# SWA bias table in 128 partitions instead of 16, and its 1 MB store from there

## The chip, the cores and the metric

The kernel runs on one core of a Trainium2 chip. The metric is the device time of one execution in microseconds. Before the change it is 2172.07 us, the median of three runs (2171.89 to 2172.37).

## The reference

One layer of a streaming encoder in float32: 1024 prompt tokens and 64 sample tokens, width 1024. A projection gives the inputs of two branches, retention (4 heads) and sliding-window attention (SWA, 16 heads, each chunk of 64 queries against 192 keys). Their gated sum is followed by cross-attention and a SwiGLU. The change is in the SWA branch's relative-position bias, which is the same for every chunk:

```python
bucket = jnp.where(rel > 0, half, 0) + jnp.where(n < max_exact, n, large)
b = table[bucket]                       # table: 32 buckets x 16 heads
s = s + bias.astype(jnp.float32)        # 16 heads x 64 queries x 192 keys
```

The bias depends only on key position minus query position, which takes 255 values. So one row of 255 numbers for each head holds all of it.

## The kernel before, in words

All large matmuls are made from a high and a low part of each operand, three products each. The projections of the first stage go through a seven-product scheme (`strassen`, with the matmuls on lines 223, 224 and 226, the DVE sums on lines 274 and 613, and the splits into parts on lines 124 and 125). Head by head, `project_phase` projects keys, queries, values and, from head 1 on, one pair of SWA query tiles (`w_sq`). It stores them in DRAM and runs `retention(h)`. This takes four blocks of 256 tokens and the 64 sample tokens. Each block loads ks, vf and qs from `d_qkv`, turns ks and vf on TensorE (line 768), makes scores `pss` (lines 157 to 159), the state's update `pkv` and the output `po`. A scheduler mixes these with the projections of the next matrix, in an order fixed when the program is built.

`bias_table` is put on the list `self.later` behind `retention(1)`, and is emitted by the next matmul group that empties this list. It does the following.

- Line 570 and 571 load the table (32 buckets by 16 heads) and a 32x256 matrix with a one in the bucket of each distance.
- Line 573 multiplies them: row h of `pb` is the bias of head h at the 255 distances.
- Line 574 scales by 8 and writes it twice in a row, into `rb`, 512 columns in 16 partitions.
- Line 575 stores it to `d_rb` in DRAM, 64 copies of the row of 256 for each head. The source is the 16 partitions, each read 32 times by a stride of zero: 512 pieces of 2 KB, 1 MB in all.
- Lines 579 to 585 spread the sinks with a further matmul.

Much later `begin_swa` (line 1116) reads `d_rb` back with a row stride of 255 instead of 256, by which each query's row is shifted by one.

Loads and stores of this stage are all issued by SP (`load`, line 118, `store`, line 121), one behind another in a fixed order. Each also waits for the DMA issued some eight before it that has the same semaphore (DMAHW0 to DMAHW7). POOL multiplies the SWA query tiles by the norm (line 619) ahead of their stores to `d_sq`, two stores for each tile: one of 128x8x64 and one of 128x32.

These are SP's rows from the bias store on, in the program before. Behind each stands what the instruction waits for; the names are the tiles of this section, and stage holds the SWA query tiles.

```order
153 L121 DMA d_rb<-rb 512x1x512 [waits DMAHW6_49,DVE_49]
154 L121 DMA d_sq<-stage_640 128x32 [waits DMAHW7_49,Pool_49]
155 L121 DMA d_sq<-stage_640 128x8x64 [waits DMAHW0_49]
156 L121 DMA d_sq<-stage_640 128x32 [waits DMAHW1_49,Pool_49]
157 L121 DMA d_sq<-stage_640 128x8x64 [waits DMAHW2_49]
158 L118 DMA vf<-d_qkv 128x2x256 [waits DMAHW3_49,PE_49]
159 L121 DMA d_sq<-stage_640 128x8x64 [waits DMAHW4_49,Pool_49]
160 L121 DMA d_sq<-stage_640 128x32 [waits DMAHW5_49]
161 L118 DMA raw<-w_q 128x1024 [waits DMAHW6_49,DVE_49]
162 L118 DMA ks<-d_qkv 128x2x256 [waits DMAHW7_49,PE_49]
163 L118 DMA qs<-d_qkv 128x2x256 [waits DMAHW0_49]
```

The load of w_q in row 161 has the semaphore of the bias store in row 153. With the change these rows read the same, each at its place.

Of the kernel before, what the change touches and what calls it, by code (L numbers as in the profile page):

```python
# [11 lines left out]
F32 = mybir.dt.float32  # L12
F32R = mybir.dt.float32r
AF = mybir.ActivationFunctionType
ALU = mybir.AluOpType
# [4 lines left out]
P = 128  # L20
# [7 lines left out]
BLK = 256  # L28
# [81 lines left out]
class Kernel:  # L110
# [453 lines left out]
    def bias_table(self):  # L564

        nc, io = self.nc, self.io
        t = self.ra.tile([P, BLK + 16], F32, tag="sf", bufs=1, name="table")
        rb = self.ra.tile([P, 2, BLK], F32, tag="o", bufs=1, name="rb")[:16]
        table, onehot = t[:32, BLK:], t[:32, :BLK]
        self.load(table, io["rel_bias"])  # L570
        self.load(onehot, io["c_onehot"])
        pb = self.norm_psum("pb")
        nc.tensor.matmul(pb[:16, :256], table, onehot, start=True, stop=True)
        nc.vector.tensor_scalar(rb, pb[:16, :256].unsqueeze(1).broadcast_to([16, 2, 256]), 8.0, None, ALU.mult)
        self.store(self.d_rb.rearrange("h (i c) -> h i c", c=512),
                   rb.rearrange("p a b -> p (a b)").unsqueeze(1).broadcast_to([16, 32, 512]))
        row = self.np.tile([P, 16], F32, tag="row", bufs=1, name="row")[:1]
        self.load(row, io["sinks"])
        ps = self.norm_psum("ps")
        nc.tensor.matmul(ps[:, :16], self.ones[:1, :], row, start=True, stop=True)  # L580
        for e in range(2):
            rows = slice(e * 64, (e + 1) * 64)
            nc.vector.tensor_copy(self.sinks[rows, :], ps[rows, :16].rearrange("p (a b) -> p a b", b=2)[:, :, e])
        self.minus = self.np.tile([P, 16], F32, tag="row", bufs=1, name="minus")[:, :NPAIR]
        nc.vector.tensor_scalar(self.minus, self.sinks, -1.0, None, ALU.mult)
# [1307 lines left out]
```

## Time and profile before

| | |
|---|---|
| median of the runs | 2172.07 us |
| profiled execution | 2170.14 us |
| its span, first to last instruction | 2168.3 us |
| mean granted clock of TensorE | 0.996 |
| PE, DVE, ACT, POOL busy | 98%, 71%, 40%, 27% |
| DMA: moved, mean rate | 290.84 MB, 134 GB/s |
| bias store issued, landed after | 306.5 us, 12.7 us |

Times in the profile are microseconds from the start of the span. PE is TensorE's matmul, PEld its loading of the stationary operand, DVE VectorE, ACT ScalarE, POOL GpSimd, and SPq the DMA issues on SP's queue. A row of the timeline has start, duration, engine, line, operation, output and inputs, and in brackets how long the engine had been idle and what released it. A row of a table of stretches has the stretch, its length, busy time of PE, PEld, DVE, ACT and POOL with the number of instructions, the granted clock, the busy share of the 16 DMA engines, and GB/s.

### The profile page before, as it was taken

The page shows a single profiled execution, that of the slowest core. Times are in us where ns is not written, and L with a number is a line of the kernel's source. Part 1 is how long each engine was busy: PE and PEld are TensorE (multiplying, and loading weights), DVE is VectorE, ACT ScalarE, POOL GpSimd, SP SyncE. Part 2 cuts the span into 40 slices and gives each one's busy share as a digit, 9 for nine tenths or more (in the row PEclk, how much of TensorE's full clock was granted, in tenths as well). Part 3 has the DMA queues.
Part 4 walks back from the last instruction along what each step waited for, and adds up shares of the span by engine and source line. Part 5 has one row for each costly group of instructions (what it writes and reads, how often), then busy time and mean ns, then how long its engine had stood idle before and what let it go on. Part 6 is the DMA issues. An engine that isn't in the chain of part 4 may idle for free. (4 is left out here: it accounts for less than half of the span.)

```text
span 2168.3 us, 41740 instructions
## 1 busy us (share of the span) xinstructions
PE 2134.6 (98%) x16371; PEld 2082.8 (96%) x16371; DVE 1547.7 (71%) x2874; ACT 875.0 (40%) x1896; POOL 588.8 (27%) x484
## 2 busy tenths in 40 slices
PE   9999999999999999999999999999999999999997
PEld 9999999999999997889999999999999999999997
DVE  8986978776677558656545565778777777877597
ACT  8333434353434357543233333333322222344243
POOL 0001211233253124540000000015556555523531
PEclk9999999999999999999999999999999999999998
DMA  7334453444345476336442121522342333384333
GB/s 268 118 128 120 135 140 104 138 126 154 120 142 178 154 228 218 119 108 209 133 147 96 40 69 46 161 67 91 126 149 89 105 117 100 117 311 151 112 116 112
DMA packets 169894, 290.84 MB, mean 134 GB/s; under 512 B 39298, under 2 KB 96546, under 8 KB 169698
## 3 DMA queue, kind: packets, MB, share of 16 engines
q1 hardware_dynamic: 161666, 269.00, 38.8%
q0 software_dynamic: 3424, 10.82, 1.4%
q10 hardware_dynamic: 4608, 8.36, 1.0%
q8 instruction: 129, 2.11, 0.4%
q14 instruction: 67, 0.55, 0.1%
HBM read 196.95 MB, written 91.16 MB: 133 GB/s over the span
## 5 line engine op out<-in xcount | busy, mean ns | idle before, releaser
L125 DVE TENSOR_TENSOR wq<-raw,wq 128x512 fp32r<-128x512 f32 (+1 forms) x499 | 435.4, 877 | 131.8 <-ACT wq L124 128.2
L124 ACT CAST wq<-raw 128x512 fp32r<-128x512 f32 (+1 forms) x499 | 301.8, 614 | 539.8 <-PE pq L226 210.5
L224 PE MATMUL pq<-T,wq 128*128 128x272 f32 x1832 | 492.2, 289 | 0.1
L223 PE MATMUL pq<-T,wq 128*128 128x272 f32 x1832 | 490.7, 288 | 1.3 <-DVE stage L613 0.6
L224 PE MATMUL pq<-B,wq 128*128 128x272 f32 x1592 | 427.0, 288 | 0.1
L223 PE MATMUL pq<-B,wq 128*128 128x272 f32 x1592 | 425.7, 288 | 0.0
L226 PE MATMUL pq<-T,wq 128*128 128x272 f32 x1832 | 382.9, 289 | 1.9 <-DVE wq L125 1.9
L223 PEld LDWEIGHTS pq<-T,wq 128*128 128x128 f32 x1832 | 344.4, 188 | 2.1 <-ACT xsq L499 0.8
L224 PEld LDWEIGHTS pq<-T,wq 128*128 128x128 f32 x1832 | 344.2, 188 | 1.2 <-issue 0.8
L226 PE MATMUL pq<-B,wq 128*128 128x272 f32 x1592 | 331.7, 289 | 0.0
L224 PEld LDWEIGHTS pq<-B,wq 128*128 128x128 f32 x1592 | 299.1, 188 | 0.8 <-issue 0.4
L223 PEld LDWEIGHTS pq<-B,wq 128*128 128x128 f32 x1592 | 299.0, 188 | 0.1
L226 PEld LDWEIGHTS pq<-T,wq 128*128 128x128 f32 x1832 | 289.8, 189 | 3.9 <-DVE wq L125 2.4
L201 POOL TENSOR_TENSOR raw<-raw 128x512 f32<-128x512 f32 (+1 forms) x44 | 62.2, 1413 | 802.4 <-DVE rs_r L322 455.6
L226 PEld LDWEIGHTS pq<-B,wq 128*128 128x128 f32 x1592 | 251.7, 189 | 0.9 <-issue 0.7
L274 DVE TENSOR_TENSOR u<-pq,u 128x544 f32<-128x544 f32 x177 | 127.2, 719 | 84.8 <-PE pq L226 84.6
L619 POOL TENSOR_TENSOR stage<-stage,rstd 128x544 f32<-128x544 f32 x20 | 31.6, 1584 | 323.0 <-ACT rstd L514 203.7
L613 DVE TENSOR_TENSOR stage<-pq,u 128x544 f32<-128x544 f32 x112 | 80.3, 718 | 31.6 <-PE pq L226 27.8
L157 PE MATMUL pd<-xc,wq 128*128 128x256 f32 (+1 forms) x256 | 74.5, 291 | 0.0
L1541 POOL TENSOR_TENSOR stage<-stage,rstd_f 128x544 f32<-128x544 f32 x40 | 63.9, 1607 | 39.1 <-ACT stage L1540 39.1
L159 PE MATMUL pd<-xc,wq 128*128 128x256 f32 (+1 forms) x256 | 74.1, 290 | 0.0
L158 PE MATMUL pd<-xc,wq 128*128 128x256 f32 (+1 forms) x256 | 73.7, 288 | 0.0
(391 smaller groups left out, 4587.2 us busy)
## 6 DMA issues: line engine op xcount, KB each, us to landing
hl<-d_op SPq DMA_DIRECT2D x85, 272.0 KB, 5.1
d_qkv<-stage SPq DMA_DIRECT2D x44, 272.0 KB, 2.2
d_op<-stage SPq DMA_DIRECT2D x44, 272.0 KB, 2.5
d_op<-ht SPq DMA_DIRECT2D x44, 272.0 KB, 3.6
raw<-w_gate SPq DMA_DIRECT2D x22, 512.0 KB, 3.5
raw<-w_up SPq DMA_DIRECT2D x22, 512.0 KB, 5.1
raw<-w_down SPq DMA_DIRECT2D x16, 512.0 KB, 4.9
d_gate<-stage ACTq DMA_DIRECT2D x28, 272.0 KB, 2.8
```

The source lines that it names most:

```text
L124: self.last_cast = self.nc.scalar.copy(hi, src).ins
L125: return self.nc.vector.tensor_tensor(out=lo, in0=src, in1=hi.bitcast(F32), op=ALU.subtract).ins
L157: mm(ps, wh, xh, start=start, stop=False)
L158: mm(ps, wh, xl, start=False, stop=False)
L159: self.last_mm = mm(ps, wl, xh, start=False, stop=stop).ins
L201: tt(out=a11, in0=a11, in1=a21, op=sub)
L223: mm(ps[:, c, :HC], w[:, 0, ks], x[:, 0, cs], start=start, stop=False)
L224: mm(ps[:, c, :HC], w[:, 0, ks], x[:, 1, cs], start=False, stop=False)
L226: self.last_mm = mm(ps[:, c, :HC], w[:, 1, ks], x[:, 0, c * HC:(c + 1) * HC], start=False, stop=stop).ins
L274: add = lambda out, a, b: nc.vector.tensor_tensor(out=out, in0=a, in1=b, op=ALU.add)
L613: nc.vector.tensor_tensor(out=o, in0=ps, in1=sb, op=ALU.add)
L1541: nc.gpsimd.tensor_tensor(out=g, in0=g, in1=r[t], op=ALU.mult)
```

## The change

The host repeats each of the 16 columns of the table eight times, so the table is 32x128. The matmul then gives 128 rows, eight alike for each head, and DVE scales them all. In the store partition 8h + r supplies four of the 32 pieces of head h. The same bytes go to the same places of `d_rb`, in the same 512 pieces of 2 KB.

```diff
-        t = self.ra.tile([P, BLK + 16], F32, tag="sf", bufs=1, name="table")
-        rb = self.ra.tile([P, 2, BLK], F32, tag="o", bufs=1, name="rb")[:16]
+        t = self.ra.tile([P, BLK + P], F32, tag="sf", bufs=1, name="table")
+        rb = self.ra.tile([P, 2, BLK], F32, tag="o", bufs=1, name="rb")
...
-        nc.tensor.matmul(pb[:16, :256], table, onehot, start=True, stop=True)
-        nc.vector.tensor_scalar(rb, pb[:16, :256].unsqueeze(1).broadcast_to([16, 2, 256]), 8.0, None, ALU.mult)
-        self.store(self.d_rb.rearrange("h (i c) -> h i c", c=512),
-                   rb.rearrange("p a b -> p (a b)").unsqueeze(1).broadcast_to([16, 32, 512]))
+        nc.tensor.matmul(pb[:, :256], table, onehot, start=True, stop=True)
+        nc.vector.tensor_scalar(rb, pb[:, :256].unsqueeze(1).broadcast_to([P, 2, 256]), 8.0, None, ALU.mult)
+        self.store(self.d_rb.rearrange("h (r i c) -> (h r) i c", r=8, i=4),
+                   rb.rearrange("p a b -> p (a b)").unsqueeze(1).broadcast_to([P, 4, 512]))
...
-    arr["rel_bias"] = a["rel_bias"]
+    arr["rel_bias"] = np.repeat(a["rel_bias"], 8, axis=1)
```

On the engines the instructions keep their number and their order. Three differ in shape. On PE, in the place shown here, the matmul of line 573 has 128 rows:

```order
 L223 MATMUL pq<-T_250,wq 128x272
 L902 MATMUL pb<-ident,ret_o 128x64 x2
-L573 MATMUL pb<-table 16x256
+L573 MATMUL pb<-table 128x256
 L224 MATMUL pq<-T_250,wq 128x272
 L226 MATMUL pq<-T_250,wq 128x272 x2
```

The neighbours are the same matmuls as before. The scaling of line 574 on DVE writes 128x512 instead of 16x512, and the load of line 570 brings 32x128 instead of 32x16.

## Prediction

> **What bounds the kernel now.** I read the page's first part, then the waits of TensorE, then the stretch around the bias table in order of time.
>
> ```profile
> PE 2134.6 (98%) x16371; PEld 2082.8 (96%) x16371; DVE 1547.7 (71%) x2874; ACT 875.0 (40%) x1896; POOL 588.8 (27%) x484
> ```
>
> TensorE is busy for 2134.6 of 2168.3 us. Only 34 us are idle, so the change can matter only where it makes or removes idle time of PE. The waits of PE, longest in total first:
>
> ```profile
> engine line waited for: us in total, times, longest us
> PE pss L1006 <- DVE nm L1016: 3.3, 3, 1.4
> PE pk L768 <- DMA ks<-d_qkv: 2.4, 1, 2.4
> ```
>
> The second row is the longest wait for a DMA in the whole run, and it happens once. In order of time it stands 18 us behind the store of the bias table:
>
> ```profile
> 324.63 0.28 PE L226 MATMUL pq<-T,wq 128*128 128x272 f32 x1
> 327.32 0.30 PE L768 MATMUL pk<-ident,ks 128*128 128x128 f32 x1 [2.41 <-DMA ks<-d_qkv]
> 327.21 0.62 ACT L124 CAST ks<-ks 128x512 fp32r<-128x512 f32 x1 [4.79 <-DMA ks<-d_qkv]
> ```
>
> PE and ACT both wait for the load of ks (retention keys, block 1 of head 2). Matmuls there start some 0.12 us apart, so the wait costs PE 327.32 - 324.63 - 0.12 = 2.6 us. Why is ks late? SP's queue, which issues the store and the load, in order:
>
> ```profile
> 306.54 0.67 SPq L121 DMA_DIRECT2D d_rb<-rb  x1
> 309.63 0.34 SPq L121 DMA_DIRECT2D d_sq<-stage  x1
> 310.02 4.56 SPq L121 DMA_DIRECT2D d_sq<-stage  x1
> 314.67 4.26 SPq L121 DMA_DIRECT2D d_sq<-stage  x2
> 319.02 0.54 SPq L118 DMA_DIRECT2D vf<-d_qkv  x1
> 319.65 1.88 SPq L121 DMA_DIRECT2D d_sq<-stage  x2
> 321.62 0.39 SPq L118 DMA_DIRECT2D raw<-w_q  x1
> 322.10 0.54 SPq L118 DMA_DIRECT2D ks<-d_qkv  x1
> 322.70 0.54 SPq L118 DMA_DIRECT2D qs<-d_qkv  x1
> ```
>
> ```profile
> L121 SPq DMA_DIRECT2D d_sq<-stage x32: 320/426/4557, 205.6 to 500.3; - x32
> ```
>
> Issuing a d_sq store takes 0.43 us as a median of 32. The two behind the bias store take 4.56 us and most of 4.26 us: SP is held while it issues them. It is let go at 319, and the bias store lands at 306.54 + 12.7 = 319.2:
>
> ```profile
> DMA to landing us min/median/max: 12.7/12.7/12.7
> 308.00:318.00 10.00, 10.00 (x81) 9.83 (x81) 8.06 (x15) 3.53 (x8) 5.08 (x3) 1.00 0.91 100
> 782.00:784.00 2.00, 2.00 (x18) 2.00 (x17) 1.39 (x2) 0.97 (x2) 0.54 (x1) 1.00 1.01 364
> ```
>
> The first row is the landing of tile rb; the other two are stretches, whose last columns are PE clock, busy share of the DMA engines, and GB/s. For 10 us the DMA engines are 0.91 busy and move only 100 GB/s, where loads elsewhere reach 364 at the same share. So the store from 16 partitions fills the DMA engines at a quarter of their rate, SP cannot get its next stores in, and ks is issued late.
>
> **The change, part by part.** *The store.* It keeps its 1 MB and its 2 KB pieces, but 128 partitions supply them. No such 1 MB store is in the trace. The nearest stores from 128 partitions:
>
> ```profile
> d_qkv<-stage SPq DMA_DIRECT2D x44, 272.0 KB, 2.2
> d_ret<-ret_t SPq DMA_DIRECT2D x16, 256.0 KB, 2.1
> ```
>
> Bounds: not under 2.1 us, and not over four such in a row, 8.4 us. At 364 GB/s, 1.05 MB take 2.9 us; a 272 KB store would take 0.8 of its 2.2 us, so 1.4 us are fixed; I take 2.9 + 1.4 = 4.3 us. The store then lands near 311 and, at the upper bound, at 315. [...]
>
> *SP's queue behind it.* What then sets each issue? POOL supplies the d_sq tiles, a DVE cast frees the buffer of w_q, and the last score matmul of block 0 frees ks:
>
> ```profile
> 311.06 1.74 POOL L619 TENSOR_TENSOR stage<-stage,rstd 128x544 f32<-128x544 f32 x1 [1.46 <-DVE stage L613]
> 313.73 1.74 POOL L619 TENSOR_TENSOR stage<-stage,rstd 128x544 f32<-128x544 f32 x1 [0.93 <-DVE stage L613]
> 317.85 0.69 DVE L125 TENSOR_TENSOR wq<-raw,wq 128x512 fp32r<-128x512 f32 x1
> 320.11 0.28 PE L159 MATMUL pss<-qs,ks 128*128 128x256 f32 x1
> ```
>
> The second pair of d_sq stores goes at 312.8, vf right after, the third pair at 315.5, w_q at 318.55 instead of 321.62, and ks at 320.4 instead of 322.10. In the program w_q also waits for the landing of the bias store, since the two share a DMA semaphore; that is over by then. At the store's upper bound of 315 the same times hold from the third pair on, so nothing hangs on its exact speed.
>
> ```profile
> DMA to landing us min/median/max: 2.8/3.9/5.1
> ```
>
> This is ks's landing around here (two loads); 5.1 is the late one, which had w_q's 512 KB issued 0.5 us ahead of it. Now w_q is 1.9 us ahead, so I take between the ends: 320.4 + 3.9 = 324.3, with 323.2 and 325.5 as bounds. PE would ask at 324.75. By the middle value the wait is gone: **-2.6 us**. By the worst, 0.75 stays: -1.85. What is late next? ACT's cast of ks and the DVE cast behind it move forward with ks, by 2.9 us, against 2.6 for PE, so they aren't. PE's waits name no other load; the engines that they name work on what PE gave them and move forward with it, so the saving is kept.
>
> *The matmul.* Its stationary operand has 128 columns instead of 16, its 256 moving columns stay.
>
> ```profile
> 305.20 0.11 PEld L573 LDWEIGHTS pb<-table 32*16 32x16 f32 x2
> 308.29 0.29 PEld L580 LDWEIGHTS ps<-row,ones 1*128 1x128 f32 x2
> ```
>
> The two weight loads grow by at most 0.29 - 0.11 = 0.18 us; at least by 0, beside the other matmuls. I take **+0.1 us**.
>
> *The rest costs nothing.* The scaling by 8 on DVE has 512 columns per partition before and after; it takes 678 ns on 16 partitions, and the 128x512 row above took 0.69 us:
>
> ```profile
> L574 DVE TENSOR_SCALAR rb<-pb x1: 678/678/678, 305.8 to 305.8; 16x512 f32<-16x512 f32 x1
> ```
>
> ```profile
> 296.68 0.78 SPq L118 DMA_DIRECT2D table<-rel_bias  x1
> ```
>
> The table's load grows from 2 to 16 KB; it is issued 8.5 us before the matmul at 305.20, which covers it. The order on all engines and the later read of the bias stay as they were.
>
> **Sum:** -2.6 + 0.1 = -2.5 us. The profiled execution took 2170.14 us (span 2168.3 and 1.8 around it) and would come to 2167.6. The runs' median is 2172.07, 1.9 above it, for a reason that the profile can't show. I carry the difference over: **2169.6 us**. From the bounds of ks (-1.85 to -2.6) and of the matmul (0 to 0.18) the forecast's own range is 2169.5 to 2170.4.
>
> **Rivals.** *1. The clock pays too.* TensorE's clock by stretches (PE busy second, clock and DMA last):
>
> ```profile
> 323.07:326.49 3.42, 1.84 (x15) 1.63 (x14) 0.97 (x2) 0.00 (x0) 0.00 (x0) 1.00 0.90 292
> 794.11:797.53 3.42, 1.60 (x20) 1.24 (x18) 2.52 (x11) 3.32 (x7) 0.00 (x0) 1.00 0.89 271
> 797.53:800.94 3.41, 3.41 (x19) 3.33 (x16) 0.00 (x0) 3.39 (x8) 1.08 (x2) 0.50 0.37 127
> ```
>
> A stretch of 3.4 us in which PE was busy for 1.60 is followed by 3.4 us at half clock; the one that holds most of our stall had 1.84 and wasn't. The stall of 2.4 us was cut by the end of a stretch. If in the timed runs these stretches lie differently, it falls into one (busy 1.0), and half clock follows over 3.4 us of dense matmuls, which costs 1.7 us more. Then the change wins 2.5 + 1.7 = 4.2 us: 2167.9. For it: the median is 1.9 above the profiled execution. Against: the three runs lie within 0.5 us, so whatever they have, they all have, and no row of this execution shows it at the stall. [...]
>
> *2. ks stays late for another reason.* If the d_sq pieces of 256 bytes themselves clog SP, or w_q's 512 KB hold ks up again, part of the stall stays; with 1.5 of 2.6 us left, 2172.07 - 1.1 + 0.1 = 2171.1. For it: the 1.88 us for two issues at 319.65, when the bias store was over. Against: the median of 0.43 us over 32 such stores, which come in the same pairs elsewhere.
>
> *3. The store doesn't get faster,* because its target in DRAM is the limit: 2172.2 with the matmul's 0.1. Against it: 272 KB go to DRAM in 2.2 us with all delays in it, at least 124 GB/s.
>
> *4. Slower: the queues crowd on few partitions.* If the DMA engines take the 512 pieces in turn, sixteen neighbours come from four partitions, since each now supplies four pieces in a row. At 16 partitions the store had 100 GB/s; four at a time, in proportion, give 25 and 42 us in place of 10.5. SP is then held 31 us longer, vf and ks with it, and PE waits: 2172.07 + 31 = 2203. It decides once the store lands later than now, over 12.7 us. Against: before, 32 neighbours come from a single partition, and taken in turn they could not have reached 100.
>
> **How the numbers follow.** Forecast 0.46; clock 0.28; part of the stall stays 0.11; no faster store 0.08; crowding 0.07. A measurement of this kernel tells 0.2% (4.3 us) from no change: faster is below 2167.7, which the clock rival reaches in nearly half of its cases: 0.13. Slower is the crowding: 0.07. The same: 0.80. The range takes in the clock rival with 0.5 us below it and the unchanged store: 2167.4 to 2172.3, which leaves out the crowding and little else.
>
> **What would show it.** In the new profile the landing of rb should be 2.1 to 8.4 us and the d_sq issues behind it under 1 us; w_q should be issued near 318.6, ks near 320.4; the wait of pk on ks, 2.4 us, should be gone, and the group of PE's waits otherwise the same. I am wrong if the landing is short and PE still stops near 324.7, if a new wait as long stands elsewhere, or if the landing stays at 12 us.

## The result, and the profile after

The changed kernel takes 2168.30 us, the median of 22 runs; the kernel before took 2172.04 in 22 runs, the three known before among them. The ratio is 0.9985 (95% interval 0.9978 to 0.9991), a gain of 2.0 to 4.8 us. The forecast was 2169.6 with a range of 2167.4 to 2172.3. The interval holds the forecast's gain of 2.5 us and the 4.2 us of the rival on the clock alike, so the times alone don't decide between these two. One profiled execution says less about the total: it took 2170.35 us (span 2168.6), as long as the one of before. So the stretch of the change has to be read by itself.

The store's landing and the busiest stretch of its transfer after the change (DMA share and GB/s are the last two columns):

```profile
DMA to landing us min/median/max: 4.5/4.5/4.5
308.50:311.20 2.70, 2.70 (x22) 2.52 (x21) 2.29 (x6) 0.62 (x1) 1.74 (x1) 1.00 0.99 379
```

It lands after 4.5 us instead of 12.7: at a DMA share of 0.99 the engines move 379 GB/s, before 100 at 0.91. SP's queue behind it, after the change, in order; the four rows behind the store are single d_sq issues:

```profile
307.23 0.58 SPq L121 DMA_DIRECT2D d_rb<-rb  x1
310.30 0.34 SPq L121 DMA_DIRECT2D d_sq<-stage  x1
310.69 0.45 SPq L121 DMA_DIRECT2D d_sq<-stage  x1
313.51 0.33 SPq L121 DMA_DIRECT2D d_sq<-stage  x1
313.89 0.43 SPq L121 DMA_DIRECT2D d_sq<-stage  x1
314.46 0.49 SPq L118 DMA_DIRECT2D vf<-d_qkv  x1
316.17 0.99 SPq L121 DMA_DIRECT2D d_sq<-stage  x2
319.25 0.34 SPq L118 DMA_DIRECT2D raw<-w_q  x1
321.09 0.37 SPq L118 DMA_DIRECT2D ks<-d_qkv  x1
```

No issue is held any more. This execution was 0.69 us later at the store than the first, so times are compared from the store on: ks is issued 321.09 - 307.23 = 13.86 us behind it, 15.56 before. ACT's cast of ks and PE at the place of the stall, and then the first rows of PE's waits:

```profile
324.40 0.62 ACT L124 CAST ks<-ks 128x512 fp32r<-128x512 f32 x1 [1.31 <-DMA ks<-d_qkv]
325.30 0.29 PE L226 MATMUL pq<-T,wq 128*128 128x272 f32 x1
325.42 0.27 PE L768 MATMUL pk<-ident,ks 128*128 128x128 f32 x1
325.45 0.36 PE L159 MATMUL po<-vb,ss 128*128 128x256 f32 x1
```

```profile
PE pss L1006 <- DVE nm L1016: 3.5, 3, 1.4
PE pq L1730 <- DVE rstd L1721: 2.4, 1, 2.4
PE pb L902 <- ACT ret_o L896: 2.3, 3, 1.1
PE pq L224 <- DVE B L125: 2.0, 5, 1.1
```

The matmul on ks follows its neighbour after 0.12 us, and the wait for its load has left the list. In its place five waits for operand parts of the last stages have entered (2.0 us in all, the longest 1.1 us near 1912). Whether they belong to the change is asked below.

### The profile page after: what moved, and what is told of

The parts are those of the page before. It is cut to its first block, busy times and chain, and to the rows that moved or that the text cites. A ratio compares the mean times of both kernels' runs of the same rounds, so it can differ in the third digit from the quotient of the medians.

```text
span 2168.6 us, 41740 instructions
## 1 busy us (share of the span) xinstructions
PE 2134.4 (98%) x16371; PEld 2082.4 (96%) x16371; DVE 1548.5 (71%) x2874; ACT 875.1 (40%) x1896; POOL 587.4 (27%) x484
```

## The experiments

My theory: a store from 16 partitions moves at 100 GB/s, fills the DMA engines, holds SP, and so brings ks 2.6 us too late. The main rivals: something else in the change gives the gain; the stall saturates; and the clock has a share in it. The runs for which no median is given were executed once each and took 2166.37 to 2176.28 us. Single executions of the kernel before differ as much (2168.59 to 2176.41), so these runs are read by their stretches and not by their times.

### The wide table, stored from 16 partitions

```diff
-    arr["rel_bias"] = np.repeat(a["rel_bias"], 8, axis=1)
+    arr["rel_bias"] = np.tile(a["rel_bias"], (1, 8))
...
-        self.store(self.d_rb.rearrange("h (r i c) -> (h r) i c", r=8, i=4),
-                   rb.rearrange("p a b -> p (a b)").unsqueeze(1).broadcast_to([P, 4, 512]))
+        self.store(self.d_rb.rearrange("h (i c) -> h i c", c=512),
+                   rb[:16].rearrange("p a b -> p (a b)").unsqueeze(1).broadcast_to([16, 32, 512]))
```

> The table is loaded, multiplied and scaled in all 128 partitions, but stored from the first 16 only, with the 32 copies of before (the host lays the 16 columns side by side eight times, so partition h still has head h). My theory, that only the source of the store matters: landing 12.5 to 12.9 us, the d_sq issues behind it held for 4 to 5 us each, PE waits 2.2 to 2.7 us for ks in block 1 of head 2. The rival, that the wider table and matmul bring the gain by some shift in time: the wait for ks is gone though the landing is 12.7.

The landing, SP's four d_sq issues in one row, and the wait in this run:

```profile
DMA to landing us min/median/max: 12.6/12.6/12.6
309.62 9.39 SPq L121 DMA_DIRECT2D d_sq<-stage  x4
PE pk L768 <- DMA ks<-d_qkv: 2.6, 1, 2.6
```

The two issues that are held take 4.57 and 3.57 us. With load, matmul and scaling in 128 partitions, but the store from 16, the whole stall is back. So the gain comes from the store's source.

### The store from 32 and from 64 partitions

The edits change the copies of each row on the host (2 and 4 for 8), the number of rows of the matmul and the scaling, and the store; for 32:

```diff
+        self.store(self.d_rb.rearrange("h (r i c) -> (h r) i c", r=2, i=16),
+                   rb.rearrange("p a b -> p (a b)").unsqueeze(1).broadcast_to([32, 16, 512]))
```

> Two rows for each head, the store from 32 partitions, 16 copies each. My theory in its simple form, rate in proportion to the partitions: 200 GB/s, 5.2 us of transfer, landing 6.5 to 7.2 us, and no wait for ks, since the store is through by 314.5. The rival that the target in DRAM was the limit and something else freed the queue: landing still over 11 us. [...]

> Four rows for each head, the store from 64 partitions, 8 copies each. If the rate goes with the number of partitions: 364 GB/s or the engines' limit, landing 4.3 to 4.8 us as from 128. The rival, that the place of the partitions counts and not their number: landing as from 32, 6.5 to 7.2 us. [...] Both: no wait of PE for ks.

Landing and rate of 32 partitions:

```profile
DMA to landing us min/median/max: 7.5/7.5/7.5
309.00:312.00 3.00, 3.00 (x25) 3.00 (x26) 2.72 (x6) 0.62 (x1) 1.53 (x2) 1.00 0.93 197
```

And of 64:

```profile
DMA to landing us min/median/max: 7.3/7.3/7.3
309.00:312.00 3.00, 3.00 (x24) 2.93 (x24) 2.58 (x7) 0.62 (x1) 1.54 (x2) 1.00 0.93 197
```

32 partitions double the rate, 197 GB/s against 100; 64 add nothing, with 197 again. The simple form, rate by the number of partitions, has fallen. Both landings are a little over the 6.5 to 7.2 us expected. Neither run has a wait of PE for ks, as the prediction said for any landing up to 8.4 us. The target in DRAM isn't what held the store at 100 GB/s, since the same bytes reach it at 197.

### Sixteen partitions, spread out

```diff
-        self.store(self.d_rb.rearrange("h (r i c) -> (h r) i c", r=8, i=4),
-                   rb.rearrange("p a b -> p (a b)").unsqueeze(1).broadcast_to([P, 4, 512]))
+        self.store(self.d_rb.rearrange("h (i c) -> h i c", c=512),
+                   rb[::8].rearrange("p a b -> p (a b)").unsqueeze(1).broadcast_to([16, 32, 512]))
```

> The table in 128 partitions as in the change, but the store takes only every eighth (0, 8, ... 120), 32 copies each: as many source partitions and copies as before the change, spread out. If the number of partitions or the 32-fold reading of a row sets the rate: landing 12.5 to 12.9 us and the wait for ks of 2.2 to 2.7 us. If their place does: about half the transfer, landing 6.2 to 7.2 us, and no wait for ks. [...]

```profile
DMA to landing us min/median/max: 7.0/7.0/7.0
309.00:312.00 3.00, 3.00 (x26) 3.00 (x25) 2.61 (x5) 0.62 (x1) 1.53 (x2) 1.00 0.93 205
```

As many partitions and as many copies as before the change, twice the rate, 205 GB/s against 100, and no wait of PE for ks. So it is the place of the source partitions that counts here, not their number and not the 32-fold reading. That the place would give about half the transfer was my estimate, which no run had shown; the landing of 7.0 us is inside its 6.2 to 7.2. The rates come in steps: 100 GB/s from partitions 0 to 15, 197 from 0 to 31 and from 0 to 63 alike, 379 from all 128. What makes the steps isn't shown.

### The slow store on another queue

```diff
-        self.store(self.d_rb.rearrange("h (i c) -> h i c", c=512),
+        nc.scalar.dma_start(self.d_rb.rearrange("h (i c) -> h i c", c=512),
```

> The kernel before, with its store from 16 partitions, but issued on ScalarE's queue instead of SP's; nothing else moves. My theory has two steps, a slow store and a held SP. With the store on another queue SP's ring should not fill: d_sq issues under 1 us, w_q issued near 318.6 and ks near 320.4, though the landing stays 12.5 us or more; the wait for ks is under 0.8 us. The rival, that the busy DMA engines delay everything whichever queue the store is on: d_sq issues of 4 us again or ks landing as late as 326 and later, wait for ks over 2 us.

The store on ScalarE's queue, what SP did behind it, and PE's wait:

```profile
306.25 0.66 ACTq L575 DMA_DIRECT2D d_rb<-rb  x1
309.33 9.30 SPq L121 DMA_DIRECT2D d_sq<-stage  x4
321.93 0.38 SPq L118 DMA_DIRECT2D ks<-d_qkv  x1
PE pk L768 <- DMA ks<-d_qkv: 1.7, 1, 1.7
```

My second step was wrong in its cause. SP is held for 9.3 us though its own queue carries none of the bias store: from 309.5 to 315 nothing but the store moved, on ScalarE's queue, with the DMA engines 0.90 busy. So the store need not stand in SP's own queue: SP's four issues took 9.30 us with it on SP's queue, in the first profile of before, and 9.30 with it on ScalarE's. By what mechanism the issue is held isn't shown. ks is issued as late as before, 15.68 us behind the store. PE's wait of 1.7 us lies between the two expectations (under 0.8, over 2): ks landed 4.2 us behind its issue here, 5.1 in the first profile of before. Why isn't shown.

### The slow store in quarters on that queue

```diff
+        for i in range(0, 32, 8): nc.scalar.dma_start(self.d_rb.rearrange("h (i c) -> h i c", c=512)[:, i:i + 8],
+                           rb.rearrange("p a b -> p (a b)").unsqueeze(1).broadcast_to([16, 8, 512]))
```

> The store from 16 partitions on ScalarE's queue, cut into four stores of 256 KB one behind another, 512 pieces of 2 KB in all as before. The order of work is that of before up to far behind the stretch. The run with one store on that queue held SP's d_sq issues just as long, so my step 'SP's own queue is full' has fallen. New theory: a DMA engine finishes its whole share of a DMA before it turns to another queue. Then d_sq gets in after the first or second quarter (2.4 us each): no d_sq issue over 5 us, the third pair before 318, and the wait for ks is under 1.2 us. [...] The rival, that the SBUF side is simply clogged for all queues while slow reads run: d_sq issues 9 us again, as with one store.

SP's four d_sq stores, then vf, and the wait; the second row is two issues, of 1.95 and 2.47 us, the later one from 312.70 to 315.2:

```profile
309.87 0.34 SPq L121 DMA_DIRECT2D d_sq<-stage  x1
310.26 4.91 SPq L121 DMA_DIRECT2D d_sq<-stage  x2
315.22 3.00 SPq L121 DMA_DIRECT2D d_sq<-stage  x1
318.31 1.67 SPq L118 DMA_DIRECT2D vf<-d_qkv  x1
PE pk L768 <- DMA ks<-d_qkv: 1.9, 1, 1.9
```

The expectation was half right. SP's issues are now held for 1.95, 2.47 and 3.00 us instead of 4.56 and 3.48, near the 2.6 us that a quarter of a megabyte takes at 100 GB/s. But one issue after another is held, vf too, the third pair comes at 320 and not before 318, and PE still waits 1.9 us where under 1.2 was expected. These steps fit the theory that an engine changes queues between DMAs; no run shows by which rule it does.

### Two stores

The first of these is the kernel before, the second the changed one, each with the store issued twice. They have the same order of work as each other, so they are compared with each other.

```diff
-        self.store(self.d_rb.rearrange("h (i c) -> h i c", c=512),
+        for _ in range(2): self.store(self.d_rb.rearrange("h (i c) -> h i c", c=512),
```

> The kernel before with its store from 16 partitions issued twice in a row (the same bytes to the same place). The scheduler orders the matmuls behind it a little otherwise, as in the next kernel, so these two are compared with each other. My theory: SP is held until both stores are through, near 329.5; ks is issued 10 us later than in the kernel before and PE stops 9 to 13 us for it or for vf. Time 8 to 13 us over the next kernel. The rival, that the stall saturates because other work fills in: under 5 us over the next one.

> The changed kernel with its store from 128 partitions issued twice in a row, in the same order of work as the kernel with two stores from 16. My theory: the second costs 2.8 us more of DMA time, through by 314.5; ks is issued within 0.5 us of when it is in the changed kernel, no wait for it over 0.5 us, and a time within 0.2% of the changed kernel. The rival, that any second megabyte holds SP: PE waits 2 us or more.

PE's wait with two stores from 16 partitions:

```profile
339.10 1.09 PE L768 MATMUL pk<-ident,ks 128*128 128x128 f32 x4 [13.09 <-DMA ks<-d_qkv]
```

In both kernels the second store is issued only when the first has landed, 12.8 us behind it from 16 partitions and 4.6 from 128. With 16, SP stands still for 4.7 us for that landing, a wait that the kernel before doesn't have; so the late ks follows the store's time here, but not by busy engines alone. With two stores from 128 there is no wait for ks, which is issued 13.87 us behind the first store. The medians are 2181.94 (9 runs) and 2167.72 (10 runs), 14.2 us apart, a little over the 8 to 13 expected. Part of that is the clock: the 2.8 us of matmuls behind the wait, up to 341.90, run at half clock (a matmul of line 223 takes 0.57 us there against 0.29 in the first profile of before), which is worth an estimated 1.4 us, half of them. Against the kernel before the ratios are 1.0043 (1.0031 to 1.0055) and 0.9977 (0.9968 to 0.9986). Once ks is late, most of the further store time lands on PE: 13.1 us of waiting instead of 2.4, for a second landing of 12.7. From 128 partitions a second megabyte costs nothing that the runs show: 2167.72 us against 2168.30 with one, in a somewhat different order of matmuls.

### The kernel before, three profiles more, and the changed one again

These four have no edit.

> The kernel before, unchanged, timed against itself and profiled a second time. It tells how far times spread with no change at all (ratio 1.000 within 0.1%), and tests the rival on the clock: if the stretches of half clock lie otherwise from run to run, this profile has half clock over 3.4 us right behind the wait for ks in two cases of three; by my forecast without it there is none, and PE waits 2.2 to 2.7 us as in the first profile.

> The kernel before, a third profile. Wait of PE for ks 2.3 to 2.7 us again. The clock: half clock over 3.4 us right behind the wait was there in two of three profiles with a landing of 12.7 us and a wait of 2.4 to 2.6 us; if it depends on where the stretches of 3.4 us lie, it comes in about two of three, and 140 matmuls of that place take 1.7 us more with it than without.

> The kernel before, a fourth profile, for the same count: half clock behind the wait for ks in two cases of three, none in the third.

> The changed kernel, a second profile. Landing 4.5 us, no wait for ks, no half clock near 327. The first profile lost 3 us in the last part of the program, at stretches that the change doesn't touch. If that is chance, this one loses another amount or none, and its stretch from the table to block 1 of head 2 is as long as in the first within 0.2 us.

Timed against itself, the kernel before gives 0.9999 (0.9987 to 1.0010). PE waited 2.6, 2.5 and 2.7 us for ks. Clock by stretches, in the second profile of before:

```profile
326.02:329.43 3.41, 1.33 (x12) 1.37 (x13) 0.28 (x1) 1.45 (x3) 0.00 (x0) 1.00 0.29 104
329.43:332.84 3.41, 3.41 (x18) 3.41 (x17) 3.41 (x7) 2.82 (x9) 0.00 (x0) 0.50 0.36 112
```

In the third, and in the fourth:

```profile
325.39:328.80 3.41, 0.99 (x9) 1.02 (x10) 0.00 (x0) 1.10 (x3) 0.00 (x0) 1.00 0.47 168
328.80:332.21 3.41, 3.41 (x18) 3.41 (x17) 3.34 (x7) 3.17 (x10) 0.00 (x0) 0.50 0.32 76
```

```profile
325.52:328.93 3.41, 0.95 (x8) 0.98 (x9) 0.00 (x0) 1.06 (x3) 0.00 (x0) 1.00 0.43 155
328.93:332.34 3.41, 3.41 (x18) 3.41 (x17) 3.30 (x7) 3.22 (x10) 0.00 (x0) 0.50 0.30 76
```

And in the changed kernel at the same place:

```profile
325.00:328.40 3.40, 3.40 (x30) 3.40 (x30) 2.82 (x5) 3.40 (x11) 0.00 (x0) 1.00 0.19 24
```

In three of four profiles of before the stall is followed by 3.4 us at half clock: 18 matmuls where the changed kernel does 30. The wide table stored from 16 partitions had it too:

```profile
323.98:327.39 3.41, 0.93 (x8) 0.71 (x6) 0.14 (x1) 0.04 (x1) 0.00 (x0) 1.00 0.74 265
327.39:330.80 3.41, 3.33 (x16) 3.36 (x17) 2.27 (x4) 3.41 (x10) 0.00 (x0) 0.50 0.01 4
```

The first profile of before, on which the prediction rests, is the odd one. What this costs is read between two fixed issues, the bias store and the load of ks for block 2, which ends the stretch in every run. First comes the load in the first profile of before, whose store was issued at 306.54; then both issues in the third of before; then both in the changed kernel's second profile:

```profile
337.04 0.36 SPq L118 DMA_DIRECT2D ks<-d_qkv  x1
```

```profile
306.99 0.67 SPq L121 DMA_DIRECT2D d_rb<-rb  x1
339.07 0.36 SPq L118 DMA_DIRECT2D ks<-d_qkv  x1
```

```profile
306.99 0.58 SPq L121 DMA_DIRECT2D d_rb<-rb  x1
334.90 0.36 SPq L118 DMA_DIRECT2D ks<-d_qkv  x1
```

| kernel, profile | store to ks of block 2, us | half clock behind the stall |
|---|---|---|
| before, first | 30.50 | no |
| before, second | 32.27 | yes |
| before, third | 32.08 | yes |
| before, fourth | 32.39 | yes |
| wide, stored from 16 | 32.16 | yes |
| from 16, on ScalarE's queue | 29.80 | no |
| the same in quarters | 31.51 | yes |
| changed, first and second | 27.91, 27.91 | no |
| from 32, 64, spread 16 | 27.93, 27.92, 27.91 | no |

Without half clock the stall costs 30.50 - 27.91 = 2.6 us; with it 4.2 to 4.5 in the kernel before and in the wide one. The two runs on ScalarE's queue, with waits of 1.7 and 1.9 us, differ by 1.7 us in the same way. Every store that landed in 4.5 to 7.5 us ends at 27.9, so a still faster one has nothing more to gain at this place.

The wait near 1912 in the first profile after isn't the change's: in the fourth profile of before the same pair of lines has 1.2 us, and in the second of the changed kernel 1.0. That execution of the changed kernel took 2168.65 us. Half clock in the later stages comes and goes in both kernels too: it begins at 797.53 in the first profile of before and at 804.42 in the first of the changed kernel, and in the second profile of either there is none between 333 and 2150.

## Why the prediction was right, and where it was short

The sign held, and the time lies in the range, 1.3 us below the forecast. By its own steps:

- *What bounds it.* Right about the wait of PE: with two stores, and so two landings of 12.7 us, it is 13.1 us long instead of 2.4. Not right about "only": in 3.41 us at half clock PE did 18 matmuls, where the changed kernel did 30 in 3.40, so more was at stake than idle time.
- *The store.* Forecast 4.3 us to landing, measured 4.5. The reason that I gave, 16 partitions as a source, is right for partitions 0 to 15 (100 GB/s), but their place counts, as the spread store showed (205).
- *SP held.* Right as the prediction has it, that the store fills the DMA engines (0.91 busy at 100 GB/s) and SP cannot get its next stores in (4.56 us for an issue). My narrower reading behind it, that the store has to be in SP's own queue, was wrong: with the store on ScalarE's queue SP was held as long, 9.3 us.
- *The issues behind it.* ks was forecast 13.86 us behind the store (320.4 less 306.54), and came at 13.86. The reasons held too: SP waits 2.0 us for the cast that frees w_q's buffer, and then 1.4 us for the score matmul that frees ks.
- *ks in time.* Right. ACT's cast of ks, which needs it, starts at 324.40, 1.0 us before PE reaches its matmul at 325.42; -2.6 us was measured as 2.6 (30.50 to 27.91). The term for ks's landing was too long: 3.9 us taken, 3.3 measured, with w_q's load now issued 1.84 us ahead instead of 0.48. ACT's cast comes 3.5 us earlier, counted from the store; 1.7 of this is the issue of ks and 1.8 its landing. What shortened the landing wasn't tested by itself.
- *The matmul.* Forecast +0.1, between 0 and 0.18. From its start to that of the next matmul it was 305.20 to 305.73 before, and 305.77 to 306.40 after, so 0.10 more. First before, then after:

```profile
305.20 0.60 PE L573 MATMUL pb<-table 32*16 32x256 f32 x2
305.73 0.40 PE L224 MATMUL pq<-T,wq 128*128 128x272 f32 x1
```

```profile
305.77 0.69 PE L573 MATMUL pb<-table 32*128 32x256 f32 x2
306.40 0.40 PE L224 MATMUL pq<-T,wq 128*128 128x272 f32 x1
```

- *The sum.* -2.5 us is what the stretch gained against the first profile of before. The median moved by 3.7; 2168.30 is nearer to the 2167.9 of the rival on the clock than to the forecast. The term that I had outside the sum, as the rival on the clock with 0.28, belongs in it with about three quarters of its size. The four profiles of before average 31.81 us from store to ks of block 2, so the mean gain there is 31.81 - 27.91 - 0.10 = 3.8 us. That this meets 3.7 so closely is chance, with an interval of 2.0 to 4.8 us and half clock that comes and goes elsewhere. The step that failed is "no row of this execution shows it at the stall", from which I gave the clock the smaller chance: one execution cannot show how often a stretch of 3.4 us takes in a stall of 2.4. My other argument against the clock, that three runs lay within 0.5 us, was chance too: 22 runs lie within 7.8. From run to run the half clock behind the stall lies differently: it begins at 327.39 (wide, stored from 16), 328.80, 328.93 and 329.43 (third, fourth and second profile of before), or not at all (the first).
- *The rivals.* No faster store, crowding and part of the stall: none came. The 1.88 us for two issues at 319.65, which I took as a sign for part of the stall staying, fell to 0.99.

## What to carry to other kernels

Here a DMA that read from 16 neighbouring partitions kept the DMA engines 0.91 busy at 100 GB/s, about a quarter of the 379 that all 128 partitions gave, and held four issues of a queue that did not carry it for 9.3 us. So a store that nobody waits for stopped TensorE for 2.4 us, 18 us later. Spreading its source over every eighth partition, or widening it to 32 or more, was enough (205, and 197 or more). In a profile this is a stretch with a high DMA share and low GB/s (here 0.91 and 100), followed by long issue times (4.56 us against a median of 0.43). A stall of TensorE like this one of some 2.4 us should be priced with the half clock that may follow it, as it did in three of four profiles of before, and from more than one profile.

## What the runs showed of the hardware

- The rate goes with the place of the partitions: 0 to 15 gave 100 GB/s, 0 to 31 and 0 to 63 both 197, every eighth of 128 gave 205, all 128 gave 379.
- A DMA issue on SP took up to 4.6 us while one slow store kept the engines busy, on SP's own queue or on another, and 5.35 behind the second of two, against a median of 0.43.
- Half clock came here without an idle stretch ahead of it. Behind the stall it followed stretches of 3.4 us in which PE was busy for 0.93 to 1.54 us, and not those with 1.73 (ScalarE's queue) and 1.84 (first profile of before). No single limit on busy time fits all runs: elsewhere it did not follow one with 1.63 (second profile of before, from 831.19), and did follow ones with 1.86 (spread sixteen, from 790.67) and 2.72 (two stores from 128, from 1348.06). What decides isn't shown.
